# A two-layer transformer trunk on one core: the head of the kernel is rearranged, and GpSimd makes every other low half of the weights in the first stage

## The chip, the core and the metric

The kernel runs on one core of a Trainium2 chip. The metric is the device time of one execution in microseconds (us). Before the change it is 995.92 us, the median of three runs (994.32 to 996.22). Five engines share the work, each with its own queue of instructions that it runs in order: TensorE (PE in the profile, with PEld for its weight loads), VectorE (DVE), ScalarE (ACT), GpSimd (POOL) and SyncE (SP), which here only starts DMA transfers.

## The reference, cut to what matters

The input is a sequence of 256 tokens with 1024 features, x, and one vector c of 1024 features. All weights are float32. Two layers follow each other, and each has a SwiGLU feed-forward block, an attention block, and a second feed-forward block. Shift, scale and gate of every block come from c (adaLN). The part of it that the change touches is the start:

```
c_act = silu(c)
mod = c_act @ ada_w[layer] + ada_b[layer]
sh1, sc1, g1, ... = split(mod, 9)
h = rms_norm(x, norm_g[layer, 0]) * (1 + sc1) + sh1
x = x + 0.5 * g1 * ((silu(h @ w_gate) * (h @ w_up)) @ w_out)
```

rms_norm divides by the root of the mean square over the 1024 features. There are 2816 hidden features, so w_gate and w_up have 1024 x 2816 elements each.

## The kernel before, in words

**Layout.** Features lie on the 128 partitions in eight chunks k = 0 to 7, tokens along the free dimension: x is a tile of 128 x 8 x 256. A product of 128x128 weights with 128x256 activations is one matmul of the profile.

**Products in three parts.** To keep float32 precision with the faster format fp32r, every weight piece `raw` (128 x 1024 floats, one DMA of 512 KB) is split in two: ScalarE writes the high half `wh` (a cast, in the helper `cp_part`, L286), and then VectorE writes the low half `wl` = raw - wh (in `sub_part`, L296). Activations are split in the same way into `HH` (ScalarE) and `HL` (VectorE). `mm3` (L396) then does three matmuls per block: wh HH, wl HH, wh HL. All the low halves are made by VectorE. Pieces are loaded in a fixed order through six `raw` buffers, and `sub_part` asks for the next piece when it has been issued.

**adaLN.** Each `ada_block` (L192) is one VectorE instruction over 128 x 1024 elements (a product with `cact` = silu(c) and a sum over the free dimension; CUSTOM_DVE_ANT_0 in the profile), followed by a short read of the accumulator and, for a scale, a tiny instruction on `modall`. Two blocks come with one DMA of 1 MB (`ada`, three buffers).

**The head** (L134 to L151 and L756 to L781). SP loads c as one row `crow`, then x in four transfers of two chunks each, then the first `ada` and `raw` tiles. PE spreads c over the partitions (`pc`), ScalarE squares x in four instructions (`sqs`) and writes `cact`, VectorE adds the squares in four instructions (the last result is `sqa`), PE sums them over partitions (`psn`), and VectorE and ScalarE turn this into 1/rms (`r`, in `rstd_of`, L446). Meanwhile VectorE has done the first two ada blocks.

**The first stage** (L555 to L571) goes over the eight chunks k of the first feed-forward block; for each there are 16 weight blocks, so 48 matmuls into eight PSUM banks (`pf`). Between the matmuls of chunk k the program issues, for the next chunk: an ada block, a cast, a second ada block, then `make_h` (L461), which is `ht` = x * scale * r on VectorE and `HH` = ht + shift on ScalarE, then a low half, a cast, `HL` on VectorE and a low half. Each chunk has two weight pieces, 2k and 2k+1. After the eighth chunk the hidden features of this part are taken out of PSUM, and the rest of the block goes on with other loops.

**What sets the order.** The class `InOrder` (L55) wraps the engines: it keeps instructions in program order on each engine and keeps a rough model of the engines' times, by which later stages decide when to issue casts, low halves and ada blocks (`bg`, L364). In the first stage the order is written out by hand. GpSimd does little before the change; its first arithmetic comes with the first attention.

Of the kernel before, what the change touches and what calls it, by code (L numbers as in the profile page):

```python
# [10 lines left out]
F32 = mybir.dt.float32  # L11
# [93 lines left out]
def trunk(ctx, tc, a, out):  # L105
# [16 lines left out]
    def sbank(name):  # L122
        return pp.tile([P, 512], F32, tag="s", name=name, bufs=2)
# [8 lines left out]


    crow = ap_.tile([P, 2, D], F32, tag="ada", name="crow").rearrange("p a b -> p (a b)")  # L134
    sp.dma_start(crow[:1, :D], a["c"])
    dve.memset(crow[:1, D:D + P], 1.0)
    vecs = cp_.tile([P, a["vecs"].shape[1]], F32, name="vecs")
    act.dma_start(vecs, a["vecs"])
    xx = cp_.tile([P, NC, S], F32, name="x")
    for k in range(0, NC, 2):  # L140
        sp.dma_start(xx[:, k:k + 2], a["x"][:, k:k + 2])
    x = [xx[:, k] for k in range(NC)]
    ones = cp_.tile([P, P], F32, name="ones")
    dve.memset(ones, 1.0 / D)
# [148 lines left out]
        act.plainly(lambda: act.copy(wh[:, :n], raw[:, :n]))  # L293
        his.append(wh)

    def sub_part():  # L296

        u = len(los)
        if u == len(his):
            return  # L300
        n = pieces[u][2]
        dve.t = max(dve.t, used[u - NLO] if u >= NLO else 0.0)
        wl = wp.tile([P, WB], F32R, tag="wl", name="wl", bufs=NLO)[:, shift.get(u, 0):]
        dve.plainly(lambda: dve.tensor_tensor(wl[:, :n], raws[u][:, :n], his[u][:, :n].bitcast(F32),
                                              op=ALU.subtract))
        los.append(wl)
        w_dma()

# [221 lines left out]
    def ffn(l, i, kind, m, nxt, at=2):  # L530

        hid = []
        nhid = [0]

        def hid_out(hf):
            j = nhid[0]
            nhid[0] += 1
            hh = cp_.tile([P, 512], F32R, tag=f"hidh{j}", name=f"hidh{j}")
            hl = cp_.tile([P, 512], F32R, tag=f"hidl{j}", name=f"hidl{j}")
            hid.append((hh, hl))  # L540
            act.copy(hh, hf)
            later(1, lambda: dve.tensor_tensor(hl, hf, hh.bitcast(F32), op=ALU.subtract))

        def evac(pg, pu):
            sg = kp.tile([P, 512], F32, tag="w512a", name="sg")
            act.activation(sg, pg, AF.Silu)

            def second():
                hf = kp.tile([P, 512], F32, tag="w512b", name="hf")
                dve.tensor_tensor(hf, sg, pu, op=ALU.mult)  # L550
                hid_out(hf)
            later(1, second)

        j0 = 0
        if (l, i) == (0, 0):  # L555
            banks = ([mmbank(f"pf{b}") for b in range(4)] + [sbank(f"pf{b}") for b in range(4, 6)]
                     + [abank("pf6"), bbank("pf7")])
            for k in range(NC):
                if k:
                    ada_block()  # L560
                    cp_part()
                    ada_block()
                f = make_h(k, kind, m)
                sub_part()
                cp_part()
                f()
                sub_part()
                blk = take("win0")
                for b in range(4 * K0):
                    mm3(banks[b // 2][:, (b % 2) * 256:(b % 2) * 256 + 256], blk(b * P), hn[k],  # L570
                        k == 0 and b % 2 == 0, k == NC - 1)  # L571
            table(AF.Silu)
            cp_part()
            sub_part()
            cp_part()
            sub_part()
            mode[0] = "run"
            for j in range(K0):
                if j < 2:
                    evac(banks[2 * j], banks[2 * j + 1])  # L580
                    if j == 0:
                        flush()
                        flush()
                else:
                    later(2 * j - 2, lambda j=j: evac(banks[2 * j], banks[2 * j + 1]))
            j0 = K0
        elif kind == "late":
            banks = [mmbank("lg0"), mmbank("lg1"), sbank("lu0"), sbank("lu1")]
            r = None
            for kh in range(2):  # L590
                blk = take("win")
                for kk in range(4):
                    k = kh * 4 + kk
                    for b in range(4):
                        mm3(banks[b][:, :SX], blk(kk * 512 + b * P), hx[k], k == 0, k == NC - 1)
                    if k == 2:
                        r = rstd_of(AF.Silu)
                        mh = MakeH(r, m)
                    elif 2 < k < 7:
                        mh.go(2 if k < 6 else 1)  # L600
            mh.go(2)
            mode[0] = "run"
            sg = kp.tile([P, 512], F32, tag="w512a", name="sg")
            hf = kp.tile([P, 512], F32, tag="w512b", name="hf")
            cols = []

            def late_out(b):
                if b == 0:
                    cols.append(late_cols(banks))
                c = cols[0]  # L610
                t = kp.tile([P, S], F32, tag="sq", name=f"lt{b}")
                dve.tensor_tensor(t, banks[b][:, :S], r, op=ALU.mult)
                cs = slice((b % 2) * S, (b % 2) * S + S)
                if b < 2:
                    act.activation(sg[:, cs], t, AF.Silu, bias=c[:, b:b + 1])
                else:
                    dve.scalar_tensor_tensor(hf[:, cs], t, c[:, b:b + 1], sg[:, cs],
                                             op0=ALU.add, op1=ALU.mult)
                if b == 3:
                    hid_out(hf)  # L620
            for b in range(4):
                later(2 + b, lambda b=b: late_out(b))
            j0 = 1
        for j in range(j0, NG):
            pg, pu = mmbank(f"pg{j}"), mmbank(f"pu{j}")
            for kh in range(2):
                blk = take("win")
                for kk in range(4):
                    k = kh * 4 + kk
                    for b in range(4):  # L630
                        mm3((pg, pu)[b // 2][:, (b % 2) * 256:(b % 2) * 256 + 256],
                            blk(kk * 512 + b * P), hn[k], k == 0 and b % 2 == 0, k == NC - 1)
                    run_laters()
            evac(pg, pu)
            if (l, i) == (0, 0) and j == K0 + 2:
                constants()
        table(AF.Abs_reciprocal_sqrt)
        gate = (l, 2 if i == 0 else 8)
        for n in range(NC):
            po = mmbank(f"po{n}")[:, :S]  # L640
            if n == NC - NFILL:
                mode[0] = "fill"
            for hf in range(2):
                blk = take("wout")
                for kk in range(11):
                    k = hf * 11 + kk
                    if n == 0 and k == 18:
                        flush()
                        flush()
                    hh, hl = hid[k // 2]  # L650
                    o = (k % 2) * 256
                    mm3(po, blk(kk * P), (hh[:, o:o + 256], hl[:, o:o + 256]), k == 0, k == 21)
                    if kk in (1, 4, 6, 9):
                        run_laters()
            need(gate)
            if nxt is not None:
                need(nxt[0]) if n >= 4 else None
            if n == NC - 1 and nxt is not None:
                need(*nxt)
                shift_cols(nxt)  # L660

            def upd(n=n, po=po):
                f = x_update(n, po, mods[gate][1], nxt, dve)
                later(1, f)
            if n < NC - 1:
                later(1, upd)
            else:
                flush()
                flush()
                upd()  # L670
                flush()
# [78 lines left out]
    def ticked(gen):  # L750
        for i, n in gen:
            if i % 2:
                run_laters()


    ada_dma(2)  # L756
    w_dma(2)
# [3 lines left out]
    w_dma()  # L761
    table(AF.Silu)
    sq4 = []
    pc = [sbank(f"pc{i}") for i in range(2)]
    for i in range(2):
        mm(pc[i], crow[:1, D:D + P], crow[:1, i * 512:(i + 1) * 512], start=True, stop=True)
    for k in range(0, NC, 2):
        sq = kp.tile([P, 512], F32, tag="w512a" if k % 4 else "w512b", name=f"sqs{k}")
        act.activation(sq, xx[:, k:k + 2].rearrange("p a b -> p (a b)"), AF.Square)
        sq4.append(sq)  # L770
    for i in range(2):
        act.activation(cact[:, i * 512:(i + 1) * 512], pc[i], AF.Silu)
    table(AF.Abs_reciprocal_sqrt)
    for i, j in ((0, 1), (2, 3), (0, 2)):
        dve.tensor_tensor(sq4[i], sq4[i], sq4[j], op=ALU.add)
    sqa = kp.tile([P, S], F32, tag="sq", name="sqa")
    dve.tensor_tensor(sqa, sq4[0][:, :S], sq4[0][:, S:], op=ALU.add)
    ada_block()
    ada_block()
    rstd = rstd_of(None, [sqa])  # L780
    cp_part()  # L781


# [583 lines left out]
```

## Time and profile before

| what | value |
|---|---|
| runs | 995.92 us median of 3 (994.32 to 996.22) |
| the profiled execution's own time | 994.77 us |
| span of its trace, first to last instruction | 993.0 us |
| mean granted TensorE clock | 0.996 |
| busy PE / DVE / ACT / POOL | 969.0 / 807.2 / 561.0 / 64.4 us |
| data moved by DMA | 265.06 MB, mean 267 GB/s |

Times in the profile count from the span's first instruction. A row of the timeline gives the start, the duration, the engine, the line of the program, the operation, what it writes and reads, the shapes and a count; in square brackets stands how long the engine had been idle and what ended that. Instructions of a helper that records them all have the line of that helper, L100, so one goes by the names of the tiles. An instruction's duration overlaps the start of the next on its engine by some hundredths of a microsecond.

### The profile page before, as it was taken

To read this page: it belongs to the slowest core of one execution; us is meant where nothing else is said; L and a number is where in the kernel's file an instruction comes from. 1 tells how busy PE (TensorE), PEld (TensorE's weight loads), DVE (VectorE), ACT (ScalarE), POOL (GpSimd) and SP (SyncE) were. 2 spreads that over 40 slices of the span, in tenths; PEclk is the share of its full clock that TensorE was granted. 3 is DMA by queue.
4 is the path that set the end of the run, shared out by engine and by line. 5 is a ranking of instruction groups with operands and counts; after the bars stand their busy time and mean duration, and the time that the engine had idled before them with its cause. 6 is when DMAs were issued, how large, how long until landed. Compare 5 with 4: busy or idle time off the path is not lost. (4 is left out here: it accounts for less than half of the span.)

```text
span 993.0 us, 20517 instructions
## 1 busy us (share of the span) xinstructions
PE 969.0 (98%) x8140; PEld 944.6 (95%) x8140; DVE 807.2 (81%) x1331; ACT 561.0 (56%) x923; POOL 64.4 (6%) x88
## 2 busy tenths in 40 slices
PE   5999999999999999999989999999999999999996
PEld 4999999988999999999988999999998999999996
DVE  7989879989899998788788998889987597555553
ACT  5465545575777654455476544545567576554552
POOL 0000100000102000000100000000038110000000
PEclk9999999999999999999999999999999999999999
DMA  9987999968766699889838899989765237554561
GB/s 352 413 341 274 331 362 342 353 207 309 266 226 228 228 392 354 302 265 326 338 120 324 317 337 339 331 305 321 279 227 182 86 107 257 195 196 150 173 179 42
DMA packets 67857, 265.06 MB, mean 267 GB/s; under 512 B 7817, under 2 KB 7969, under 8 KB 57650
## 3 DMA queue, kind: packets, MB, share of 16 engines
q1 hardware_dynamic: 65666, 258.31, 72.8%
q0 software_dynamic: 1664, 4.81, 1.6%
q8 instruction: 63, 1.03, 0.4%
q10 hardware_dynamic: 432, 0.64, 0.2%
q14 instruction: 32, 0.26, 0.1%
HBM read 262.66 MB, written 2.65 MB: 267 GB/s over the span
## 5 line engine op out<-in xcount | busy, mean ns | idle before, releaser
L100 DVE TENSOR_TENSOR wl<-raw,wh 128x1024 fp32r<-128x1024 f32 (+1 forms) x368 | 401.2, 1105 | 92.0 <-issue 25.1
L100 ACT CAST wh<-raw 128x1024 fp32r<-128x1024 f32 (+1 forms) x368 | 348.5, 958 | 204.8 <-PE pu L100 99.9
L100 DVE CUSTOM_DVE_ANT_0 ada<-ada,cact,vecs 128x1024 f32<-128x1024 f32 x160 | 203.2, 1278 | 0.0
L100 PE MATMUL po<-hidl,wh 128*128 128x256 f32 x704 | 194.4, 276 | 0.0
L100 PE MATMUL po<-hidh,wh 128*128 128x256 f32 x704 | 194.3, 276 | 0.0
L100 PE MATMUL po<-hidh,wl 128*128 128x256 f32 x704 | 194.3, 276 | 0.0
L100 PE MATMUL pg<-HH,wl 128*128 128x256 f32 x608 | 168.2, 277 | 0.0
L100 PE MATMUL pg<-HH,wh 128*128 128x256 f32 x608 | 168.2, 277 | 0.0
L100 PE MATMUL pu<-HH,wh 128*128 128x256 f32 x608 | 168.1, 276 | 0.0
L100 PE MATMUL pu<-HL,wh 128*128 128x256 f32 x608 | 168.1, 276 | 0.0
L100 PE MATMUL pg<-HL,wh 128*128 128x256 f32 x608 | 168.1, 276 | 0.0
L100 PE MATMUL pu<-HH,wl 128*128 128x256 f32 x608 | 168.0, 276 | 0.0
L100 PEld LDWEIGHTS po<-hidl,wh 128*128 128x128 f32 x704 | 132.1, 188 | 0.0
L100 PEld LDWEIGHTS po<-hidh,wh 128*128 128x128 f32 x704 | 132.1, 188 | 0.0
L100 PEld LDWEIGHTS po<-hidh,wl 128*128 128x128 f32 x704 | 132.1, 188 | 0.0
L100 PEld LDWEIGHTS pg<-HH,wh 128*128 128x128 f32 x608 | 114.1, 188 | 0.7 <-ACT tri L100 0.6
L100 PEld LDWEIGHTS pg<-HH,wl 128*128 128x128 f32 x608 | 114.1, 188 | 0.0
L100 PEld LDWEIGHTS pg<-HL,wh 128*128 128x128 f32 x608 | 114.2, 188 | 0.0
L100 PEld LDWEIGHTS pu<-HH,wh 128*128 128x128 f32 x608 | 114.2, 188 | 0.0
L100 PEld LDWEIGHTS pu<-HH,wl 128*128 128x128 f32 x608 | 114.1, 188 | 0.0
L100 PEld LDWEIGHTS pu<-HL,wh 128*128 128x128 f32 x608 | 114.1, 188 | 0.0
L100 ACT ACTIVATE HH<-ht,modall 128x256 fp32r<-128x256 f32 x56 | 27.8, 507 | 40.5 <-DVE ht L100 36.4
(214 smaller groups left out, 1619.9 us busy)
## 6 DMA issues: line engine op xcount, KB each, us to landing
raw<-in_win SPq DMA_DIRECT2D x176, 512.0 KB, 6.3
ada<-in_ada SPq DMA_DIRECT2D x79, 1024.0 KB, 7.5
raw<-in_wout SPq DMA_DIRECT2D x64, 384.0 KB, 4.8
raw<-in_wout SPq DMA_DIRECT2D x64, 320.0 KB, 4.9
raw<-in_wqk SPq DMA_DIRECT2D x16, 512.0 KB, 6.2
raw<-in_wo SPq DMA_DIRECT2D x16, 512.0 KB, 5.4
raw<-in_wv SPq DMA_DIRECT2D x8, 512.0 KB, 9.0
raw<-in_wkk SPq DMA_DIRECT2D x8, 512.0 KB, 7.8
```

The lines of the kernel that those rows point to most:

```text
L100: return self.tc.keep_in_program_order(f(*args, **kw))
```

## The change

Five edits in the head and one in the first stage:

1. c is loaded by ScalarE's queue, ahead of `vecs` (the small vectors), where SP loaded it ahead of x.
2. x comes in two transfers of four chunks (512 KB) where there were four of two.
3. ScalarE squares the first four chunks in two instructions, VectorE the last four in two (x times x).
4. GpSimd adds the first two tiles of squares, VectorE does two adds; the last add (`sqa`) goes, and PE sums the two halves of `sqs` by two products into `psn`.
5. A new function `warm` issues matmuls of the tile `ones` with itself into a PSUM bank that nobody reads: three ahead of `pc`, three behind it, six behind `psn`.
6. In the first stage, for k = 1 to 7, the low half of piece 2k is issued to GpSimd ahead of `make_h`, where VectorE made it behind `ht`. VectorE still makes the low half of piece 2k+1, and both of chunk 0.

```diff
-    sp.dma_start(crow[:1, :D], a["c"])
+    act.dma_start(crow[:1, :D], a["c"])
...
-    for k in range(0, NC, 2):
-        sp.dma_start(xx[:, k:k + 2], a["x"][:, k:k + 2])
+    for k in range(0, NC, 4):
+        sp.dma_start(xx[:, k:k + 4], a["x"][:, k:k + 4])
...
-    def sub_part():
+    def sub_part(pool=False):
...
+        if pool:
+            nc.gpsimd.tensor_tensor(wl[:, :n], raws[u][:, :n], his[u][:, :n].bitcast(F32), op=ALU.subtract)
+        else:
+            dve.plainly(lambda: dve.tensor_tensor(wl[:, :n], raws[u][:, :n], his[u][:, :n].bitcast(F32),
+                                                  op=ALU.subtract))
...
                     ada_block()
                     cp_part()
                     ada_block()
+                if k:
+                    sub_part(pool=True)
                 f = make_h(k, kind, m)
-                sub_part()
+                if not k:
+                    sub_part()
                 cp_part()
                 f()
                 sub_part()
...
+    def warm(n):
+
+        pw = bbank("warm")
+        for _ in range(n):
+            mm(pw[:, :P], ones, ones, start=True, stop=True)
...
+    warm(3)
     pc = [sbank(f"pc{i}") for i in range(2)]
...
-        act.activation(sq, xx[:, k:k + 2].rearrange("p a b -> p (a b)"), AF.Square)
+        xk = xx[:, k:k + 2].rearrange("p a b -> p (a b)")
+        if k < 4:
+            act.activation(sq, xk, AF.Square)
+        else:
+            dve.tensor_tensor(sq, xk, xk, op=ALU.mult)
...
-    for i, j in ((0, 1), (2, 3), (0, 2)):
+    nc.gpsimd.tensor_tensor(sq4[0], sq4[0], sq4[1], op=ALU.add)
+    for i, j in ((2, 3), (0, 2)):
         dve.tensor_tensor(sq4[i], sq4[i], sq4[j], op=ALU.add)
-    sqa = kp.tile([P, S], F32, tag="sq", name="sqa")
-    dve.tensor_tensor(sqa, sq4[0][:, :S], sq4[0][:, S:], op=ALU.add)
+    warm(3)
     ada_block()
     ada_block()
-    rstd = rstd_of(None, [sqa])
+    rstd = rstd_of(None, [sq4[0][:, :S], sq4[0][:, S:]])
+    warm(6)
     cp_part()
```

Two places of the program show what the prediction rests on. The first is VectorE in the first stage, one turn of the loop over chunks, from one `ht` to the next (`ht` the scaled activations, `wl` a low half of weights, `HL` the low half of the activations, `ada` an adaLN block). Before:

```order
L100 SCALAR_TENSOR_TENSOR ht_228<-x,modall,r_143 128x256
L100 TENSOR_TENSOR wl<-raw,wh 128x1024
L100 SCALAR_TENSOR_TENSOR HL<-ht_228,modall,HH 128x256
L100 TENSOR_TENSOR wl<-raw,wh 128x1024
L100 ISA ada,modall<-ada,cact,vecs 128x1024
L100 ISA modall 128x1
L100 SCALAR_TENSOR_TENSOR modall<-modall,vecs 128x1
L100 ISA ada,modall<-ada,cact,vecs 128x1024
L100 ISA modall 128x1
L100 SCALAR_TENSOR_TENSOR ht_297<-x,modall,r_143 128x256
```

One low half has gone from between `ht` and `HL`, so that `HL` follows `ht` at once. The same turn of VectorE now:

```order
L100 SCALAR_TENSOR_TENSOR ht_244<-x,modall,r_148 128x256
L100 SCALAR_TENSOR_TENSOR HL<-ht_244,modall,HH 128x256
L100 TENSOR_TENSOR wl<-raw,wh 128x1024
L100 ISA ada,modall<-ada,cact,vecs 128x1024
L100 ISA modall 128x1
L100 SCALAR_TENSOR_TENSOR modall<-modall,vecs 128x1
L100 ISA ada,modall<-ada,cact,vecs 128x1024
L100 ISA modall 128x1
L100 SCALAR_TENSOR_TENSOR ht_313<-x,modall,r_148 128x256
```

All else of the turn stands as it stood. The second place is GpSimd from the head to the end of the first stage; before the change nothing stands here but the start of a small DMA:

```order
L1036 DMA fb<-in_fgb 16x1
L791 ISA
L791 TENSOR_TENSOR sqs_122<-sqs_122,sqs_124 128x512
L305 TENSOR_TENSOR wl<-raw,wh 128x1024 x7
L824 DMA udram<-ut 8x383
```

The add of squares and the seven low halves are what GpSimd has gained, each with two inputs in SBUF. ScalarE's order in the stage is unchanged: HH of a chunk, then two casts.

More of the change, by code (lines that the diff above doesn't have):

```diff
@@ L303, in sub_part @@
         wl = wp.tile([P, WB], F32R, tag="wl", name="wl", bufs=NLO)[:, shift.get(u, 0):]
-        dve.plainly(lambda: dve.tensor_tensor(wl[:, :n], raws[u][:, :n], his[u][:, :n].bitcast(F32),
-                                              op=ALU.subtract))
+        if pool:
[3 more added lines that the diff above has]
+                                                  op=ALU.subtract))
         los.append(wl)
```

## The prediction

> **What bounds the kernel now.** I read the page first, then who waited for whom on PE, then the timeline of the first stage engine by engine, because all edits lie ahead of its end. PE is busy nearly all the time, and the waits on PE behind 62 us say whether later stages can give back or swallow a shift:
>
> ```profile
> PE 969.0 (98%) x8140; PEld 944.6 (95%) x8140; DVE 807.2 (81%) x1331; ACT 561.0 (56%) x923; POOL 64.4 (6%) x88
> PE pk L100 <- ACT HH L100: 2.7, 1, 2.7
> PE s L100 <- ACT qk L100: 1.3, 3, 0.9
> PE psn L100 <- ACT sq L100: 0.6, 1, 0.6
> ```
>
> Behind 62 us PE waits for under 6 us in all, and each time for a result that hangs on PE's own earlier work. So I take a shift of the first stage's end to reach the end of the kernel in full. That stage on PE:
>
> ```profile
> 15.05 0.58 PE L100 MATMUL pf<-HH,wh 128*128 128x256 f32 x1 [3.76 <-ACT HH L100]
> 17.06 0.41 PE L100 MATMUL pf<-HH,wh 128*128 128x256 f32 x1
> 17.28 0.41 PE L100 MATMUL pf<-HH,wl 128*128 128x256 f32 x1
> 19.62 0.34 PE L100 MATMUL pf<-HH,wh 128*128 128x256 f32 x1
> 21.07 0.28 PE L100 MATMUL pf<-HH,wh 128*128 128x256 f32 x1
> 21.18 0.28 PE L100 MATMUL pf<-HH,wl 128*128 128x256 f32 x1
> 55.98 0.28 PE L100 MATMUL pf<-HH,wl 128*128 128x256 f32 x1
> 56.27 0.38 PE L100 MATMUL pf<-HL,wh 128*128 128x256 f32 x1
> 61.79 0.27 PE L100 MATMUL pg<-HH,wh 128*128 128x256 f32 x1
> ```
>
> The stage lasts from 15.05 to 61.79 us. Matmuls start 0.21 to 0.22 us apart at first and 0.11 us apart later: PE begins at half speed, until about 19.6. A chunk takes it 48 x 0.113 = 5.4 us at full speed. Slow at first, it lags behind the engines that feed it, and catches up in the last chunk: at 56.27 it waits for the last HL. What feeds it has a turn of its own. VectorE from one `ht` to the next, and ScalarE beside it:
>
> ```profile
> 25.46 0.48 DVE L100 SCALAR_TENSOR_TENSOR ht<-x,modall,r 128x256 f32<-128x256 f32 x1
> 25.86 1.22 DVE L100 TENSOR_TENSOR wl<-raw,wh 128x1024 fp32r<-128x1024 f32 x1
> 26.99 0.47 DVE L100 SCALAR_TENSOR_TENSOR HL<-ht,modall,HH 128x256 fp32r<-128x256 f32 x1
> 27.46 1.23 DVE L100 TENSOR_TENSOR wl<-raw,wh 128x1024 fp32r<-128x1024 f32 x1
> 28.60 1.28 DVE L100 CUSTOM_DVE_ANT_0 ada<-ada,cact,vecs 128x1024 f32<-128x1024 f32 x1
> 29.92 0.16 DVE L100 SCALAR_TENSOR_TENSOR modall<-modall,vecs 128x1 f32<-128x1 f32 x1
> 30.00 1.28 DVE L100 CUSTOM_DVE_ANT_0 ada<-ada,cact,vecs 128x1024 f32<-128x1024 f32 x1
> 31.21 0.48 DVE L100 SCALAR_TENSOR_TENSOR ht<-x,modall,r 128x256 f32<-128x256 f32 x1
> ...
> 25.97 0.51 ACT L100 ACTIVATE HH<-ht,modall 128x256 fp32r<-128x256 f32 x1 [2.71 <-DVE ht L100]
> 26.39 2.00 ACT L100 CAST wh<-raw 128x1024 fp32r<-128x1024 f32 x2
> 31.72 0.51 ACT L100 ACTIVATE HH<-ht,modall 128x256 fp32r<-128x256 f32 x1 [3.33 <-DVE ht L100]
> ```
>
> A turn is 31.21 - 25.46 = 5.75 us, longer than PE's 5.4, so in the long run the turn decides. VectorE is full in it, but a second chain is exactly as long: `ht` at 25.46, HH at 25.97, the first of two casts at 26.39, over after half of 2.00 us at 27.4, and only then can the second low half start, at 27.46. From there to the next `ht` is 3.75 us of low half and ada blocks.
>
> **The low half on GpSimd, without contention: nothing.** VectorE loses one `wl`, 26.99 - 25.86 = 1.13 us a turn. But the remaining `wl` still waits for `ht`, HH and the cast: 2.00 us from `ht` to `wl`, 3.75 us from there to the next `ht`, 5.75 us as before. VectorE's freed time becomes two waits of about half a microsecond, ahead of HL and of `wl`. GpSimd's input is ready when the second cast ends, 26.39 + 2.00 = 28.4, while the next chunk needs it after 32; that cover hides up to 3.5 us of GpSimd's work. Behind GpSimd's wait only its own later work is queued, a small DMA that the program issues only in the stages behind; SP's next `raw` transfer now waits for GpSimd's read, with three turns in hand.
>
> **With contention: this is the sum.** Where GpSimd already does arithmetic, VectorE and GpSimd stand in each other's way:
>
> ```profile
> 306.52 0.74 POOL L440 TENSOR_TENSOR acc<-acc,sq 128x256 f32<-128x256 f32 x1 [0.53 <-ACT sq L100]
> 306.96 0.58 DVE L100 SCALAR_TENSOR_TENSOR HL<-x,modall,HH 128x256 fp32r<-128x256 f32 x1
> 802.30 0.80 POOL L440 TENSOR_TENSOR acc<-acc,sq 128x256 f32<-128x256 f32 x1
> 802.60 0.78 DVE L100 SCALAR_TENSOR_TENSOR HL<-x,modall,HH 128x256 fp32r<-128x256 f32 x1
> 762.00 1.25 DVE L100 TENSOR_TENSOR wl<-raw,wh 128x1024 fp32r<-128x1024 f32 x1
> 762.15 1.89 POOL L1102 TENSOR_SCALAR d<-fkb,Fq 128x256 f32<-128x256 f32 x1
> 764.61 0.91 POOL L1102 TENSOR_SCALAR d<-fkb,Fq 128x256 f32<-128x256 f32 x1
> 747.88 3.69 DVE L100 TENSOR_TENSOR wl<-raw,wh 128x1024 fp32r<-128x1024 f32 x3 [1.13 <-ACT wh L100]
> 748.03 2.92 POOL L1102 TENSOR_SCALAR d<-fkb,Fq 128x256 f32<-128x256 f32 x1
> ```
>
> HL takes 0.47 us alone. Started 0.44 us into a GpSimd add it takes 0.58 (0.11 more); started 0.30 us into one it takes 0.78 (0.31 more). In both cases its delay ends at the same point, 0.19 us ahead of the add's end (306.96 + 0.11 = 307.07 against 307.26; 802.60 + 0.31 = 802.91 against 803.10). So VectorE's instruction stands still until the add has nearly finished. The other way round, GpSimd's 128x256 instruction takes 0.91 us alone and 1.89 when a `wl` started just ahead of it: it waits for that to end. In the first stage nearly every instruction of VectorE (`ht`, HL, `wl`, ada) reads two tiles in SBUF, as HL and `wl` do. The Trainium skill, SBUF — State Buffer, section "SBUF: two separate sides", says the same as a rule: GpSimd and a VectorE operation with two SBUF inputs share a port pair as an exclusive lock for the whole instruction, and the loser blocks fully. The trace agrees, up to the last 0.19 us; by that rule alone the sum below would come out the same.
>
> How long is GpSimd's low half of 128x1024? No such row exists. Four times 0.74 is 2.96, if all of it grows with the size; if a third of a microsecond is fixed, it is 0.3 + 4 x 0.44 = 2.1. I take 2.4, and keep both ends. The Trainium skill, GPSIMD Engine Reference, section 3.1, gives 4497 ns for 2048 elements; half of it, an estimate from that page, is 2.25 us, which would make the sum below 1 us smaller.
>
> GpSimd asks at 28.4 us of the turn shown, when VectorE's `wl` runs and two ada blocks follow. It gets in at the first seam: between `wl` and ada, or at the tiny `modall` instruction at 29.92, which waits for the block before it. From then VectorE stands for 2.4 - 0.19 = 2.2 us, less 0.15 for the seam. None of that coincides with the new waits behind `ht`, which come later. So each of the seven turns from `ht` of chunk 0 to `ht` of chunk 7 grows by 2.05 us: 7 x 2.05 = 14.35 us. In the last chunk HL now follows HH at once, some 0.5 us sooner behind `ht` than before: -0.6 with the wait at 56.27. PE would idle about 2.3 us of each 7.8, and this is what an idle stretch does to its clock:
>
> ```profile
> 504.44:507.85 3.41, 1.47 (x9) 1.12 (x9) 3.08 (x9) 2.11 (x5) 0.00 (x0) 1.00 0.81 267
> 507.85:511.27 3.42, 3.42 (x16) 3.42 (x17) 3.31 (x8) 1.62 (x4) 0.00 (x0) 0.50 0.10 41
> ```
>
> With 1.47 us of work in 3.41 (second column), PE had clock 0.50 (the column behind POOL's) for the next 3.42. In a middle chunk such a dip costs PE 1.7 us of the 2.3 it idles anyway; in the last it would reach the end. I put 0.3.
>
> **The head: nothing.** The path to the first `ht` before:
>
> ```profile
> 5.84 1.25 ACT L100 ACTIVATE sqs<-x 128x512 f32<-128x512 f32 x2 [0.79 <-DMA x<-in_x]
> 7.49 0.63 ACT L100 ACTIVATE sqs<-x 128x512 f32<-128x512 f32 x1 [0.40 <-DMA x<-in_x]
> 9.94 1.28 DVE L100 CUSTOM_DVE_ANT_0 ada<-ada,cact,vecs 128x1024 f32<-128x1024 f32 x1
> 13.97 0.48 DVE L100 SCALAR_TENSOR_TENSOR ht<-x,modall,r 128x256 f32<-128x256 f32 x1
> ```
>
> The second half of x landed by 5.84, the rest by 7.49. Without c ahead of it and in fewer transfers, x ends perhaps 0.4 to 0.9 us sooner, 6.6 to 7.1. VectorE then does four instructions of 512 columns where it did three, one of them early, and a short one: about 4 x 0.6 = 2.4 us, so ada starts at 9.0 to 9.5 instead of 9.94. Against that stands GpSimd's add of squares, 128x512 with two inputs, 1.2 to 1.5 us by the bounds above, which blocks VectorE's squares: 9.9 to 10.5. I take no gain; ends -0.7 and +0.6. c moves one issue ahead of `vecs`, which is first read by the ada block, so nothing waits. The unread products raise PE's clock earlier: some (19.62 - 15.05) / 0.22 = 20 matmuls at 0.11 instead of 0.22, 2 us of PE's time. But PE waits for VectorE's turns, so this is worth nothing as long as these are longer than 5.4 us; and if the six behind `psn` run at half speed, they can end near the first matmul's old start, up to 1 us late, hidden in the same way.
>
> **Sum.** 14.35 - 0.6 + 0.3 + 0 = 14.0 us on the profiled execution's 994.77 (span 993.0), so 1008.8. The median of the runs is 1.15 above that execution: 995.92 + 14.0 = **1009.9 us**. With GpSimd's 2.1 us it is 7 x 1.75 - 0.3 = 12, so 1008; with 2.96 it is 7 x 2.6 - 0.3 = 18, so 1014. A difference under 0.2%, 2 us, is about what can't be told from none.
>
> **Rivals.**
> - *GpSimd is kept out until VectorE pauses.* The rows at 747.88 speak for it: GpSimd asked at 748.03, and two `wl` in a row went ahead. Then it gets in only behind `ht`, at 31.5, blocks HL until 33.7, and `wl` starts at 34.1 instead of 33.2: 0.9 us in each of six turns, and 0.9 in the last chunk's HL, 6.3 us: 1002.2. With the shorter GpSimd time 1000.5. Against it: three seams come earlier.
> - *No blocking that costs.* GpSimd's reads fit beside VectorE's. The turn stays 5.75, the last HL comes earlier: -0.6, 995.3, no change to be told. The four rows above speak against it.
> - *Faster.* The turn falls to PE's 5.4 us, since the clock is up at the start and VectorE has 1.13 us less: 7 x 0.33 = 2.3, with 0.6 for the end and 0.7 for the head 3.6: 992.3. It decides if the cast is done by the time HL is, that is, if `wl` no longer waits for HH on ScalarE; the order on ScalarE is unchanged, which speaks against it. The Trainium skill, TensorE: Matmul & The Clock Gate, section "Part 1", has it that about 3.4 us of steady work release the full clock; the slow stretch from 15.05 to 19.62 agrees roughly, and by that rule the unread products would end it before 15.
> - *Worse.* GpSimd's instruction is over 2.7 us long, or PE's clock falls in every turn and PE's 5.4 + 1.7 becomes the turn with the port's delays on top: up to 1016.
> - *The products do not raise the clock:* it changes nothing while VectorE's turn decides.
>
> **Chances.** Forecast 0.56, kept out 0.20, worse 0.05, no blocking 0.13, faster 0.06. The range of 1000 to 1016 holds the first three, 0.81. Faster by over 0.2% 0.06, within 0.2% 0.13, slower 0.81.
>
> **What would show it.** Right: turns of 7.6 to 8.1 us from `ht` to `ht` in the first stage; a `wl` on GpSimd of 2.1 to 3 us, with a VectorE instruction beside it that lasts 2 us longer than alone; PE idle 2 us per chunk, its first matmul near 15 us. Wrong: turns of 5.75 or less with GpSimd's `wl` beside VectorE's instructions at their old lengths, or a shift at 62 us that is gone by the end.

## The result and the profile after

The changed kernel takes 1010.88 us (median of 4, 1010.78 to 1013.54), the kernel before beside it 995.38 us (median of 4). The ratio is 1.0153, 95% interval 1.0136 to 1.0171: slower by 15.5 us, 1.5%. The profiled execution took 1010.86 us against 994.77, 16.1 us more.

All of it arises in the first stage. PE's first and last rows of that stage in the timeline of the changed kernel (`pg` is the first matmul behind it):

```profile
15.16 0.38 PE L100 MATMUL pf<-HH,wh 128*128 128x256 f32 x1 [0.91 <-ACT HH L100]
77.98 0.28 PE L100 MATMUL pg<-HH,wh 128*128 128x256 f32 x1
```

The stage begins at 15.16 us (15.05 before) and is over at 77.98 (61.79 before), 16.2 us later; the whole execution is 16.1 us later. What PE waits for behind the stage is about as much as before, 4.7 us in all against 5.3, so the shift goes through. The two longest of its waits after 78 us (in all, how often, the longest):

```profile
PE pk L100 <- ACT HH L100: 2.5, 1, 2.5
PE s L100 <- ACT qk L100: 0.7, 1, 0.7
```

One turn of VectorE in the timeline, from `ht` to `ht`, with the GpSimd low half that falls into it and ScalarE's chain beside it:

```profile
29.84 0.48 DVE L100 SCALAR_TENSOR_TENSOR ht<-x,modall,r 128x256 f32<-128x256 f32 x1
30.89 0.48 DVE L100 SCALAR_TENSOR_TENSOR HL<-ht,modall,HH 128x256 fp32r<-128x256 f32 x1 [0.58 <-ACT HH L100]
31.83 1.23 DVE L100 TENSOR_TENSOR wl<-raw,wh 128x1024 fp32r<-128x1024 f32 x1 [0.45 <-ACT wh L100]
32.97 3.42 DVE L100 CUSTOM_DVE_ANT_0 ada<-ada,cact,vecs 128x1024 f32<-128x1024 f32 x1
36.44 0.16 DVE L100 SCALAR_TENSOR_TENSOR modall<-modall,vecs 128x1 f32<-128x1 f32 x1
36.51 1.27 DVE L100 CUSTOM_DVE_ANT_0 ada<-ada,cact,vecs 128x1024 f32<-128x1024 f32 x1
37.72 0.48 DVE L100 SCALAR_TENSOR_TENSOR ht<-x,modall,r 128x256 f32<-128x256 f32 x1
...
32.82 2.49 POOL L305 TENSOR_TENSOR wl<-raw,wh 128x1024 fp32r<-128x1024 f32 x1 [5.39 <-ACT wh L100]
...
30.35 0.51 ACT L100 ACTIVATE HH<-ht,modall 128x256 fp32r<-128x256 f32 x1 [5.48 <-DVE ht L100]
30.77 1.98 ACT L100 CAST wh<-raw 128x1024 fp32r<-128x1024 f32 x2
```

The turn is 37.72 - 29.84 = 7.88 us where it was 5.75. GpSimd asks when the second cast ends (30.77 + 1.98 = 32.75) and starts at 32.82, in the last tenths of `wl`. The ada block behind that `wl` lasts 3.42 us where it takes 1.28 alone, 2.14 more; in all seven turns it lasts 3.39 to 3.43. It lies still until 32.97 + 2.14 = 35.11; GpSimd's instruction ends at 35.31, 0.2 us later, the same distance as in the small adds of the kernel before. If it lies still at its start, as the arithmetic assumes, it starts 0.15 us behind GpSimd's instruction and is free 0.2 us ahead of its end. VectorE's two new waits, 0.58 ahead of HL and 0.45 ahead of `wl`, show where its freed time went. On PE the stage shows up as a wait in each chunk:

```profile
PE pf L100 <- ACT HH L100: 11.6, 8, 1.9
```

0.9 us of it lie ahead of the first chunk, so each later one waits 1.5 us on average, where the prediction had 2.3.

The last `ht` of the stage, from VectorE's timeline (54.20 before):

```profile
69.44 0.48 DVE L100 SCALAR_TENSOR_TENSOR ht<-x,modall,r 128x256 f32<-128x256 f32 x1
```

And this is the end of the stage by windows (PE's work is the second column, its granted clock stands behind POOL's column):

```profile
68.31:71.72 3.41, 1.47 (x10) 1.07 (x9) 2.33 (x6) 1.75 (x3) 0.00 (x0) 1.00 0.42 77
71.72:75.13 3.41, 3.41 (x19) 3.41 (x18) 2.34 (x3) 3.40 (x5) 0.00 (x0) 0.50 0.99 413
```

PE worked for 1.47 us of the first window and then had half the clock in the next, in the middle of the last chunk, where no later wait hides it: about half of 3.41, 1.7 us. The same had happened once in the middle of the stage: 1.67 us of work from 44.41 to 47.83 us, clock 0.50 from 47.83 to 51.24. There VectorE's turn stayed at 7.91 us, and the dip only took time in which PE would have waited.

The head in the timeline, in the order VectorE, GpSimd, PE:

```profile
6.32 2.12 DVE L100 TENSOR_TENSOR sqs<-x 128x512 f32<-128x512 f32 x2 [5.17 <-DMA x<-in_x]
9.88 1.27 DVE L100 CUSTOM_DVE_ANT_0 ada<-ada,cact,vecs 128x1024 f32<-128x1024 f32 x1
14.08 0.48 DVE L100 SCALAR_TENSOR_TENSOR ht<-x,modall,r 128x256 f32<-128x256 f32 x1
...
6.03 1.26 POOL L791 TENSOR_TENSOR sqs<-sqs,sqs 128x512 f32<-128x512 f32 x1 [4.06 <-ACT sqs L100]
...
11.89 2.37 PE L100 MATMUL warm<-ones 128*128 128x128 f32 x12
16.37 0.28 PE L100 MATMUL pf<-HH,wh 128*128 128x256 f32 x1
16.49 0.28 PE L100 MATMUL pf<-HH,wl 128*128 128x256 f32 x1
```

x was complete at 6.32 us (7.49 before), but GpSimd had begun its add at 6.03, and VectorE's two squares lasted 2.12 us together, where two of its adds of that size took 1.42 before; the ada block began at 9.88 instead of 9.94. The unread products did what they were there for: matmuls are 0.12 us apart from 16.37 on, where they were 0.21 until 19.62. The stage could not use it.

### The profile page after: what moved, and what is told of

Read it like the earlier page. It is cut to its first block, busy times and chain, and to the rows that moved or that the text cites. A ratio compares the mean times of both kernels' runs of the same rounds, so it can differ in the third digit from the quotient of the medians.

```text
span 1009.1 us, 20579 instructions
## 1 busy us (share of the span) xinstructions
PE 980.5 (97%) x8166; PEld 953.2 (94%) x8166; DVE 816.6 (81%) x1324; ACT 559.4 (55%) x921; POOL 81.2 (8%) x96
## 3 DMA queue, kind: packets, MB, share of 16 engines
q8 instruction: 64, 1.05, 0.4%
## 5 line engine op out<-in xcount | busy, mean ns | idle before, releaser
L100 DVE TENSOR_TENSOR wl<-raw,wh 128x1024 fp32r<-128x1024 f32 (+1 forms) x361 | 392.8, 1103 | 95.3 <-issue 26.0
L100 DVE CUSTOM_DVE_ANT_0 ada<-ada,cact,vecs 128x1024 f32<-128x1024 f32 x160 | 218.2, 1371 | 0.0
```

Of the source, the lines that this page charges most:

```text
L100: return self.tc.keep_in_program_order(f(*args, **kw))
```

## The experiments

Nine kernels were run, each beside runs of the kernel before on the same chip. The medians of the kernel before in these groups lie between 995.46 and 996.92 us.

**The head alone.** The changed kernel with the old order in the first stage:

```diff
-                if k:
-                    sub_part(pool=True)
                 f = make_h(k, kind, m)
-                if not k:
-                    sub_part()
+                sub_part()
```

> The change without its edit in the first stage: c on ScalarE's queue, x in two loads, squares on two engines, unread products, but VectorE makes all low halves as before. Theory (VectorE's turn of 5.75 us in the first stage decides, so an earlier full clock of TensorE is worth nothing): first ht at 14.1 us, seven turns of 5.75 us, stage's end 61.3 to 61.9 us, time within 1 us of the kernel before, 995.4. Rival (the head is worth the 2 us of TensorE's slow matmuls): stage's end below 60 us, 993.

It took 994.21 us (median of 12), ratio 0.9987, interval 0.9977 to 0.9998. The timeline, last `ht` of the stage and first matmul behind it:

```profile
54.19 0.48 DVE L100 SCALAR_TENSOR_TENSOR ht<-x,modall,r 128x256 f32<-128x256 f32 x1
...
61.60 0.28 PE L100 MATMUL pg<-HH,wh 128*128 128x256 f32 x1
```

The last `ht` stands at 54.19 (54.20 before), the end of the stage at 61.60 (61.79). The clock was up from the fourth matmul on, and the first chunk took PE 6.3 us where it took 8.1. But each of the other seven took 5.75 us on average, which is VectorE's turn, where PE had caught up at 5.4 before. The rival falls; the head's edits are worth 0.2 us in the stage. The ratio says 1.3 us (0.2 to 2.3), of which the stage shows only that part; where the rest comes from, if it is there, these runs don't show.

**The stage alone.** The kernel before with `sub_part(pool=True)` for k > 0 and nothing of the head.

> The kernel before with the edit in the first stage alone: GpSimd makes the low half of every even piece from 2 to 14, head as before. Theory (the port between GpSimd and VectorE is the whole of the loss): turns of 7.85 to 7.95 us, one ada block of 3.4 us in each, time 1009.5 to 1011.5. Rival (the head's edits carry part of the loss): 1006 or less.

It took 1009.91 us (median of 4), ratio 1.0150, interval 1.0130 to 1.0169. One ada block of the timeline and the `ht` of the turn:

```profile
24.88 3.42 DVE L100 CUSTOM_DVE_ANT_0 ada<-ada,cact,vecs 128x1024 f32<-128x1024 f32 x1
...
29.63 0.48 DVE L100 SCALAR_TENSOR_TENSOR ht<-x,modall,r 128x256 f32<-128x256 f32 x1
```

The same 3.42 us, and the whole loss. The rival falls.

**An unread subtraction beside the old kernel.** VectorE does all that it did; GpSimd subtracts besides, into a tile for nobody.

```diff
+            spare = [cp_.tile([P, 512], F32, tag=f"hidh{j}", name=f"spare{j}") for j in (9, 10)]
...
+                if k:
+                    u = len(los)
+                    for j in range(2):
+                        cs = slice(512 * j, 512 * j + 512)
+                        nc.gpsimd.tensor_tensor(spare[j], raws[u][:, cs], his[u][:, cs].bitcast(F32), op=ALU.subtract)
                 f = make_h(k, kind, m)
```

> The kernel before, all low halves on VectorE as they were, and beside them in each of the seven turns GpSimd subtracts the same wh from the same raw in two instructions of 128x512 into a tile that nobody reads. Theory (GpSimd's reads block VectorE's instructions with two SBUF inputs, whoever needs the result): VectorE loses 2 x (1.26 - 0.19) = 2.1 us in each turn, turns of 7.7 to 8.1 us, time 1009 to 1012. Rival (the loss is a wait for GpSimd's late result): turns of 5.75 us, 995.4.

It took 1010.5 us (median of 4), ratio 1.0146, interval 1.0121 to 1.0172. VectorE's turn from the second `wl` on, then GpSimd's two instructions (from two windows of its timeline):

```profile
32.90 1.23 DVE L100 TENSOR_TENSOR wl<-raw,wh 128x1024 fp32r<-128x1024 f32 x1
34.04 2.33 DVE L100 CUSTOM_DVE_ANT_0 ada<-ada,cact,vecs 128x1024 f32<-128x1024 f32 x1
36.41 1.15 DVE L100 SCALAR_TENSOR_TENSOR modall<-modall,vecs 128x1 f32<-128x1 f32 x1
...
33.95 1.34 POOL L568 TENSOR_TENSOR spare<-raw,wh 128x512 f32<-128x512 f32 x1 [4.19 <-ACT wh L100]
35.26 2.29 POOL L568 TENSOR_TENSOR spare<-raw,wh 128x512 f32<-128x512 f32 x1
```

Nobody reads GpSimd's result, and the loss is there in full. The first half holds up the ada block by 2.33 - 1.28 = 1.05 us. The second waits until that block is over (2.29 us instead of some 1.3) and then holds up the tiny `modall` instruction, 1.15 us instead of 0.16. Both VectorE instructions are free again 0.15 to 0.2 us ahead of GpSimd's end. Both seams that the prediction named let GpSimd in. The turn is 7.78 us. The rival, a wait for a late result, falls.

**Half of it.** The same with `range(1)`: one subtraction of 128x512 in each turn.

> As the run with unread subtractions, but one of 128x512 in each turn instead of two. Theory (the loss goes with the length of GpSimd's instruction): 1.07 us more in each turn, turns of 6.8 us, time 1002.5 to 1004. Rival (a fixed loss for each meeting): as much as with two, 1009 or more, or next to nothing.

It took 1001.37 us (median of 4), ratio 1.0063, interval 1.0039 to 1.0086. The rows of VectorE and GpSimd:

```profile
27.22 0.48 DVE L100 SCALAR_TENSOR_TENSOR ht<-x,modall,r 128x256 f32<-128x256 f32 x1
30.36 2.33 DVE L100 CUSTOM_DVE_ANT_0 ada<-ada,cact,vecs 128x1024 f32<-128x1024 f32 x1
34.02 0.48 DVE L100 SCALAR_TENSOR_TENSOR ht<-x,modall,r 128x256 f32<-128x256 f32 x1
...
30.27 1.34 POOL L568 TENSOR_TENSOR spare<-raw,wh 128x512 f32<-128x512 f32 x1 [5.46 <-ACT wh L100]
```

The turn is 6.80 us, 1.05 more: half the subtraction, half the loss in the turn. The time came out about 1 us under the expected figures.

**A copy in place of the subtraction.** GpSimd copies `wh` in two instructions of 128x512: one input in SBUF.

```diff
-                        nc.gpsimd.tensor_tensor(spare[j], raws[u][:, cs], his[u][:, cs].bitcast(F32), op=ALU.subtract)
+                        nc.gpsimd.tensor_copy(spare[j], his[u][:, cs].bitcast(F32))
```

> As the run with two unread subtractions, but GpSimd copies wh in two instructions of 128x512, one SBUF input where there were two. Theory (VectorE stands as long as GpSimd reads or its instruction lasts, so the loss follows the copy's length less some 0.2 us): turns longer by the two copies' lengths less 0.4 us; a copy of 0.7 to 1.2 us gives 6.7 to 7.7 us, time 1002 to 1009. Rival (only two GpSimd instructions with two inputs take the port): turns of 5.75 to 5.9 us, 995.4 to 996.5.

It took 999.75 us (median of 10), ratio 1.0038, interval 1.0021 to 1.0055. A turn of VectorE in the timeline, then GpSimd's two copies (from two windows):

```profile
26.67 0.47 DVE L100 SCALAR_TENSOR_TENSOR ht<-x,modall,r 128x256 f32<-128x256 f32 x1
29.81 1.63 DVE L100 CUSTOM_DVE_ANT_0 ada<-ada,cact,vecs 128x1024 f32<-128x1024 f32 x1
31.48 0.44 DVE L100 SCALAR_TENSOR_TENSOR modall<-modall,vecs 128x1 f32<-128x1 f32 x1
33.05 0.47 DVE L100 SCALAR_TENSOR_TENSOR ht<-x,modall,r 128x256 f32<-128x256 f32 x1
...
29.71 0.66 POOL L568 COPY spare<-wh 128x512 f32<-128x512 f32 x1 [4.17 <-ACT wh L100]
30.31 1.60 POOL L568 COPY spare<-wh 128x512 f32<-128x512 f32 x1
```

Both expectations miss in their numbers: the turn is 6.38 us instead of 5.75, neither over 6.7 nor under 5.9. The rows show which mechanism holds. The first copy takes 0.66 us, half as long as a subtraction of that size (1.34). The ada block beside it starts 0.10 us later and loses 0.35 us (1.63 against 1.28), so it is free at 30.16, 0.21 us ahead of the copy's end at 30.37. The second copy waits for that block, as the second subtraction did: its 1.60 us are mostly this wait, for the block lasts until 31.44. It ends at 31.91, and `modall`, started at 31.48, loses 0.28 us and is free 0.15 us ahead of that. So with one input VectorE is held up in the same way as with two, until the last 0.15 to 0.2 us of GpSimd's instruction. The theory had the mechanism and took the copy too long (0.7 to 1.2 us); the rival, that a copy with one input doesn't hold VectorE up, falls.

**No low half at all.** The changed kernel, with the work that GpSimd had been given left out.

```diff
+        if pool:
+            los.append(his[u])
+            w_dma()
+            return
```

> The changed kernel, but nobody makes the seven low halves that GpSimd made: the products that would use them take the high half once more, so that part of the computation is left out. TensorE has as many matmuls. Theory (without contention the edit is worth nothing, since ScalarE's chain from ht over HH and the cast to the other low half is as long as VectorE's work was): turns of 5.7 to 5.8 us, VectorE waiting about 0.5 us ahead of HL and ahead of wl, time 994.3 to 995.5. Rival (VectorE's work alone sets the turn): turns of 5.4 to 5.5 us, set by TensorE, stage's end near 59.5 us, 993 or less.

It took 994.28 us (median of 11), ratio 0.9992, interval 0.9980 to 1.0004: no difference that can be told. A turn, and the last `ht` with the first matmul behind the stage:

```profile
25.60 0.48 DVE L100 SCALAR_TENSOR_TENSOR ht<-x,modall,r 128x256 f32<-128x256 f32 x1
...
27.61 1.23 DVE L100 TENSOR_TENSOR wl<-raw,wh 128x1024 fp32r<-128x1024 f32 x1 [0.46 <-ACT wh L100]
...
31.35 0.48 DVE L100 SCALAR_TENSOR_TENSOR ht<-x,modall,r 128x256 f32<-128x256 f32 x1
...
54.34 0.48 DVE L100 SCALAR_TENSOR_TENSOR ht<-x,modall,r 128x256 f32<-128x256 f32 x1
...
61.28 0.28 PE L100 MATMUL pg<-HH,wh 128*128 128x256 f32 x1
```

31.35 - 25.60 = 5.75 us, although VectorE has 1.13 us less to do and GpSimd nothing. Even a GpSimd that cost VectorE nothing could not have shortened the turn. The rival falls. Only the end of the stage gains: 61.28 - 54.34 = 6.94 us from the last `ht`, 7.59 before. That is the 0.6 us that the prediction gave for the earlier HL of the last chunk.

**And the cast ahead of HH.** As above, with the second `cp_part` issued ahead of `make_h`, so that the chain over ScalarE is cut.

> As the run without these low halves, and the second cast of each chunk is issued on ScalarE ahead of HH, so that wl no longer waits for ht and HH; the same part of the computation is left out. Theory (two chains of 5.75 us, and both must be shortened to reach TensorE's 5.4): turns of 5.2 to 5.5 us, TensorE without idle time in the stage, stage's end 59.0 to 60.0 us, time 992.4 to 993.6. Rival (something else, DMA or the buffers, holds the turn at 5.75): as without the change in the order of the casts, 995.

It took 994.88 us (median of 12), ratio 0.9993, interval 0.9983 to 1.0004. The timeline: two early matmuls, a turn of VectorE and the first matmul behind the stage:

```profile
18.58 0.40 PE L100 MATMUL pf<-HH,wl 128*128 128x256 f32 x1
18.80 0.30 PE L100 MATMUL pf<-HL,wh 128*128 128x256 f32 x1
...
24.94 0.48 DVE L100 SCALAR_TENSOR_TENSOR ht<-x,modall,r 128x256 f32<-128x256 f32 x1
...
30.14 0.48 DVE L100 SCALAR_TENSOR_TENSOR ht<-x,modall,r 128x256 f32<-128x256 f32 x1
...
62.40 0.28 PE L100 MATMUL pg<-HH,wh 128*128 128x256 f32 x1
```

And a window of the stage (PE's work and the count of its matmuls come second):

```profile
20.00:60.00 40.00, 40.00 (x342) 40.00 (x341) 33.19 (x55) 21.83 (x26) 0.00 (x0) 1.00 1.02 414
```

The turn fell to 5.20 us, as the theory has it, so it was ScalarE's chain that had held it at 5.75 in the run before. But the stage ended at 62.40, not at 59 to 60, and the time was not under 993.6. PE was busy without a gap, and only slower: 342 matmuls in 40 us are 0.117 us each, 5.6 us for a chunk, and in this execution they were still 0.22 us apart at 18.58, in spite of the unread products. Half of the theory, that PE would need 5.4 us, was wrong for this execution.

**The clock at the start, where PE is the bound.** The last kernel with ten unread products behind `psn` instead of six:

```diff
-    warm(6)
+    warm(10)
```

> The run without the seven low halves and with the second cast ahead of HH (the same part of the computation left out), and ten unread products behind psn instead of six, so that TensorE has no pause of 0.9 us ahead of the stage. In that run TensorE, not VectorE, set the stage's end at 62.4 us, with slow matmuls until 18.83 us and 0.118 us from matmul to matmul. Theory (TensorE is the bound there, and its clock at the start is now worth time): full clock before 16 us, turns of 5.2 us, stage's end 60.3 to 61.0 us at 0.118 us a matmul, 58.8 to 59.5 at 0.113. Rival (the slow start was not what held it): stage's end above 61.8 us.

It took 993.44 us (median of 12), ratio 0.9979, interval 0.9964 to 0.9993. Start and end of the stage on PE:

```profile
15.20 0.38 PE L100 MATMUL pf<-HH,wh 128*128 128x256 f32 x1 [0.26 <-ACT HH L100]
...
16.41 0.29 PE L100 MATMUL pf<-HH,wh 128*128 128x256 f32 x1
16.54 0.28 PE L100 MATMUL pf<-HH,wl 128*128 128x256 f32 x1
...
61.29 0.27 PE L100 MATMUL pg<-HH,wh 128*128 128x256 f32 x1
```

With the clock up from the start the stage ends 1.1 us sooner than in the last run, at 61.29; the expected 61.0 was missed by 0.3, the rival's 61.8 not reached. (61.29 - 15.20) / 384 is 0.12 us a matmul, start included.

**The same ten behind the head alone.** `warm(10)` in the run with the head's edits.

> The head's edits alone, with ten unread products behind psn instead of six; all low halves on VectorE. Theory (VectorE's turns of 5.75 us set the stage, so the clock at its start is worth next to nothing): stage's end 61.2 to 61.9 us, time within 1 us of the run with the head's edits alone. Rival (the clock at the start is worth 2 us): stage's end below 60 us.

It took 994.94 us (median of 12), ratio 0.9986, interval 0.9975 to 0.9998, and the stage ended where it had with six:

```profile
61.60 0.28 PE L100 MATMUL pg<-HH,wh 128*128 128x256 f32 x1
```

So the clock at the start is worth 1.1 us when PE is the bound, and nothing when VectorE is. Two kernels with the full computation are a little ahead of the kernel before, the head's edits with six and with ten unread products, both by 0.1% with an interval that ends just short of 1. Their profiled executions, with the same end of the stage, took 992.66 and 995.85 us; one wait behind the stage, for `pk`, was 1.3 us in the first and 3.2 in the second. So a gain of this size can't be put down to the head by these traces.

## Why the prediction was right, point by point

- **The sign and the mechanism.** Shown: the loss is there without the head, it is there when nobody reads GpSimd's result, and it halves with half the subtraction. The rule of the Trainium skill that the prediction cited (SBUF — State Buffer, "SBUF: two separate sides") holds here up to the last 0.15 to 0.2 us of GpSimd's instruction: beside subtractions of 2.49 and 1.34 us VectorE lost 2.14 and 1.05, beside a copy of 0.66 us 0.35, and GpSimd in its turn waited for an ada block. The other half, that VectorE's freed time is worth nothing, is shown by the run without the seven low halves: its turn stays at 5.75 us.
- **GpSimd's time.** Taken as 2.4 us between 2.1 and 2.96; 2.48 to 2.55 us measured.
- **Seven turns.** Predicted 7 x 2.05 = 14.35 us. Measured from the first `ht` to the eighth: (69.44 - 14.08) - (54.20 - 13.97) = 15.1, or 2.16 a turn. GpSimd got in at the first seam named. The two deductions, 0.19 at GpSimd's end and 0.15 for the seam, came out (2.49 - 0.2 - 0.15 = 2.14 in the turn shown); the 0.1 us a turn that the sum lacked is GpSimd's instruction, 2.52 us on average instead of 2.4.
- **The last chunk.** Predicted -0.6 for the earlier HL and +0.3 for the clock. Measured from the last `ht` to the end of the stage: (77.98 - 69.44) - (61.79 - 54.20) = +0.95. The -0.6 was right, as the run without the seven low halves shows (-0.65). But a dip of the clock fell into this chunk and cost about 1.6 us (0.95 + 0.65), not 0.3. It was the term furthest off: the prediction priced such a dip at 1.7 us, but took only 0.3 for the chance that it would lie in the last chunk.
- **The head.** Predicted 0 between -0.7 and +0.6; +0.1 measured at the first `ht` (14.08). x came 1.2 us sooner, more than thought, and VectorE took it back: from there to the ada block it needed 3.56 us for four instructions of 512 columns, where ScalarE's last square, two adds and a short one had taken 2.45. Some 0.7 of this 1.1 is the time that its squares lost beside GpSimd's add (1.26 us, within the 1.2 to 1.5 given).
- **The sum.** 14.0 predicted for the profiled execution, 0.1 + 15.1 + 0.95 = 16.2 found; 1009.9 us predicted and 1010.88 measured. That the times lie within 1 us is in part luck: the medians are 15.5 us apart where 14.0 were predicted, and the kernel before came out at 995.38 beside the changed one, where the prediction started from 995.92.
- **Rivals.** GpSimd kept out until VectorE pauses: wrong, it got in ahead of the first ada block in each turn shown; why two `wl` in a row went ahead at 748 us in the kernel before stays open. No blocking that costs: wrong. Faster: wrong in its condition twice over, since VectorE's turn stayed at 5.75 with no low half at all, and PE's 5.4 us for a chunk, read off a stretch with 0.113 us between matmuls, was 5.6 in the two executions where PE did set the pace.

## What to carry to other kernels

Work moved to GpSimd is not free because GpSimd is idle. In these runs its subtraction, and a mere copy too, held up the VectorE instruction beside it, which read two tiles, until 0.2 us before its own end; VectorE instructions with one input were not tried. And it needed twice VectorE's time, so VectorE lost 2.1 us for the 1.1 us it gave away. Before an engine's work is lightened, look for a second chain of the same length beside it; here HH and the cast on ScalarE made VectorE's freed time into waits. An experiment that simply leaves the work out tells in one run what the best possible outcome of moving it is.

## What the runs showed of the hardware that was not expected

- GpSimd's copy of 128x512 with one input takes 0.66 us and holds up VectorE's ada block by 0.35; its subtraction of that size takes 1.34 us and holds it up by 1.05. Both leave VectorE free some 0.2 us ahead of their end.
- At full clock, matmuls of 128x256 were 0.113 us apart in the prediction's stretch of the kernel before, and 0.118 from 18.8 us to the end of the stage in the run without GpSimd's low half and with the cast first. Both occur within one execution: in the kernel before 0.118 in the last chunk, from 57 to 61 us; with the head's edits alone 0.113 from 28 to 32 us and 0.118 from 34 to 38. The granted clock was 1.00 in all of these; what makes the difference is open.
- With the same six unread products behind `psn`, matmuls were 0.12 us apart from the stage's fourth one on in two of the four kernels that were profiled with them, one execution each, and not before 18.8 us in the other two; with ten it was so in both. The dip at the end of the stage lasted one window of 3.41 us.
